# Seven block products in place of eight for one quad of k-tiles in layer A's input projection

## The chip, the cores and the metric

The kernel runs on one core of a Trainium2 chip. Its time is device microseconds for one execution; three runs of the kernel before gave 1843.43 to 1845.11 us, median 1844.06.

## The reference, cut to what matters

A trunk of two layers on 256 rows of 2048 numbers, all in float32. The change lies in the first part of layer A:

```python
h = rms_norm(x, a_norm[layer])                     # (1, 256, 2048)
q, k, v, g = jnp.split(h @ a_w_in[layer], 4, axis=-1)   # a_w_in: (2048, 16384)
o = chunked_relbias_attention(split_heads(q), split_heads(k), split_heads(v), rel_bias)
x = x + (o * jax.nn.silu(g)) @ a_w_out[layer]      # 32 heads of 128
```

Layer B follows with two more projections of 2048 to 8192, its own attention and a projection back.

## The kernel before, in words

**Products in three parts.** A float32 product is made of three matmuls on fp32r operands. Both factors are split into a high part (the value rounded to fp32r) and a low part (the rest): h·hi, h·lo and l·hi are summed in PSUM (`mm3`, line 160). The stationary operand is a 128x128 block of the transposed activations (`xTh`, `xTl`), the moving one a 128x512 block of weights.

**Units and pairs.** The projection's columns are cut into units of 512, and the 256 rows into NT = 2 tiles, so a unit has two accumulators of one PSUM bank each. Layer A has 16 pairs of units, one for two heads each: `aqk` (q and k of the two heads) and `avg` (v and gate). A unit runs over 16 k-tiles of 128, two to a step (KB = 2): 8 steps of 12 matmuls.

**The feed.** `Feed` (line 171) brings weights to TensorE. SP loads a step's weights (128 x 2 x 512, 512 KB) into one of three `raw` buffers; ScalarE copies it to `hi` (line 216), VectorE subtracts to get `lo` (line 217). `hi` and `lo` have four buffers each, and `get` prepares three steps ahead: the `hi` of a step can be written when TensorE is done with the step four before it.

**Attention beside the products.** While one pair is multiplied, the attention of the pair before it advances in pieces between the steps (`drive`, line 519, with QK_STEPS and PV_STEPS: at which step how many pieces). Its pieces in order: the evacuation of `aqk` to `qk`; a transpose by 32x32 blocks on VectorE into `qkY` and 16 DMAs from there to `qkZ`, issued by GpSimd (`turn`, line 321); the splits `wideh`/`widel` and `q1h`/`q1l` (lines 344, 345); the scores `s1p` and `s0p` on TensorE, at the end of the `avg` unit; softmax (lines 378 to 388); the scaled gate and a second `turn` (`sgY`, `sgZ`); the split of the probabilities, again `wideh`/`widel`; the products `op` (lines 349 to 351 and 405); `oT`, and its split into `oAh` and `oAl`, the stationary operand of the output projection.

Before, the second split comes with the last step of the next pair's `aqk` unit, and `op` after the first step of that pair's `avg` unit. `qkZ` and `sgZ` share one buffer, `qkY` and `sgY` another.

**What sets the order.** The code says what depends on what; a scheduler then orders each engine's instructions by its own estimate of times, so that instructions can stand far from where the code has them. On the chip ScalarE, VectorE, SP and GpSimd each take theirs in that order; one that waits holds up all behind it.

## Time and profile before

| | |
|---|---|
| median of 3 runs | 1844.06 us |
| the profiled execution's own time | 1843.38 us |
| its span, first to last instruction | 1841.7 us |
| TensorE, matmuls | 8387, busy 1830.1 us |
| VectorE | busy 1121.7 us |
| ScalarE | busy 1005.6 us |
| GpSimd | busy 543.5 us, nearly all in issuing DMAs |
| DMA | 396.31 MB, mean 215 GB/s |

A row of a timeline has start and length in us, engine, line, instruction, out<-in, shape, how often, and in brackets the idle time of the engine before it with what ended it. Matmuls overlap each other, so the length of one is not what it costs; for that a stretch of many is divided by their number. Names lose the number of the pair: `aqk_lo` is the low part of any step of any `aqk` unit.

### The profile page before, as it was taken

What the parts mean: (1) busy time and instruction counts of PE and PEld (TensorE: products, weight loads), DVE (VectorE), ACT (ScalarE), POOL (GpSimd) and SP (SyncE); (2) the same over time, 40 slices, a digit from 0 to 9 for tenths busy, and PEclk for the clock granted to TensorE, in tenths of its full rate; (3) what the DMA queues carried; (4) which work ended last, traced back from release to release, by engine and by line L of the source; (5) the groups of instructions that cost most, each with busy time, mean ns of one, the idle gap of its engine ahead of it and who ended that gap; (6) DMA issues with size and microseconds to landing.
All of it is one profiled execution on the core that took longest, in us unless ns stands there. A gap on an engine that the chain in (4) does not pass through costs nothing.

```text
span 1841.7 us, 25094 instructions
## 1 busy us (share of the span) xinstructions
PE 1830.1 (99%) x8387; PEld 1523.0 (83%) x8387; DVE 1121.7 (61%) x1433; ACT 1005.6 (55%) x1695; POOL 543.5 (30%) x1127
## 2 busy tenths in 40 slices
PE   9999999999999999999999999999999999999998
PEld 7888888888888888888888888888888888888886
DVE  6666666666666666556655566666665666665654
ACT  6555555555555555454546565555555655554443
POOL 1333333333333333111103333333333333333000
PEclk9999999999999999999999999999999999999999
DMA  7766666666767666677756666666766766677664
GB/s 255 235 217 214 212 214 215 214 213 212 216 214 214 215 214 214 209 226 227 230 190 220 214 216 213 214 214 215 217 212 213 220 213 210 215 237 220 206 205 161
DMA packets 142241, 396.31 MB, mean 215 GB/s; under 512 B 31104, under 2 KB 35744, under 8 KB 141984
## 3 DMA queue, kind: packets, MB, share of 16 engines
q1 hardware_dynamic: 106960, 354.25, 61.6%
q0 software_dynamic: 34048, 39.13, 6.5%
q8 instruction: 66, 1.08, 0.3%
q10 hardware_dynamic: 1104, 1.34, 0.2%
q14 instruction: 63, 0.52, 0.1%
HBM read 351.05 MB, written 4.23 MB: 193 GB/s over the span
## 4 chain that ended last, share of the span: by engine, by line
PE 97%; DVE 1%; DMA 1%; ACT 0%; issue 0%; ACTq 0%; SPq 0%; DVEq 0%
PE bkv_acc L168 19%; PE bqg_acc L168 19%; PE avg_acc L168 18%; PE aqk_acc L168 18%; PE bo_acc L168 9%; PE ao_acc L168 9%; PE op L405 1%; PE s0p L371 1%; PE op L351 0%; PE s1p L351 0%; PE s1p L350 0%; PE op L350 0%; PE op L349 0%; PE s1p L349 0%; DMA avg_raw<-in_a_w_in 0%; DMA xr<-in_x_t 0%
## 5 line engine op out<-in xcount | busy, mean ns | idle before, releaser
L330 POOL DMA_DIRECT2D sgZ<-sgY x512 | 251.5, 498 | 435.2 <-DVE sgY L326 364.1
L330 POOL DMA_DIRECT2D qkZ<-qkY x504 | 247.9, 499 | 399.1 <-DVE vl L424 147.2
L217 DVE TENSOR_TENSOR bqg_lo<-bqg_raw,bqg_hi 128x1024 fp32r<-128x1024 f32 x128 | 156.0, 1222 | 121.3 <-ACT bqg_hi L216 121.3
L217 DVE TENSOR_TENSOR avg_lo<-avg_raw,avg_hi 128x1024 fp32r<-128x1024 f32 x127 | 154.0, 1219 | 110.8 <-ACT avg_hi L216 105.4
L217 DVE TENSOR_TENSOR bkv_lo<-bkv_raw,bkv_hi 128x1024 fp32r<-128x1024 f32 x128 | 155.6, 1219 | 87.6 <-ACT bkv_hi L216 87.6
L216 ACT ACTIVATE bqg_hi<-bqg_raw 128x1024 fp32r<-128x1024 f32 x128 | 135.3, 1058 | 128.3 <-PE bqg_acc L168 67.8
L217 DVE TENSOR_TENSOR aqk_lo<-aqk_raw,aqk_hi 128x1024 fp32r<-128x1024 f32 x125 | 151.5, 1219 | 84.6 <-ACT aqk_hi L216 84.5
L168 PE MATMUL aqk_acc<-aqk_hi,xTh 128*128 128x512 f32 x512 | 195.8, 392 | 0.5 <-ACT aqk_hi L216 0.5
L168 PE MATMUL bkv_acc<-bkv_hi,xkvh 128*128 128x512 f32 x512 | 195.7, 392 | 0.0
L168 PE MATMUL avg_acc<-avg_hi,xTh 128*128 128x512 f32 x512 | 195.7, 392 | 0.0
L168 PE MATMUL bqg_acc<-bqg_hi,xbh 128*128 128x512 f32 x512 | 195.5, 392 | 0.0
L216 ACT ACTIVATE avg_hi<-avg_raw 128x1024 fp32r<-128x1024 f32 x127 | 133.1, 1057 | 113.3 <-PE avg_acc L168 54.2
L168 PE MATMUL aqk_acc<-aqk_lo,xTh 128*128 128x512 f32 x512 | 194.1, 389 | 0.5 <-DVE aqk_lo L217 0.5
L168 PE MATMUL avg_acc<-avg_lo,xTh 128*128 128x512 f32 x512 | 194.1, 389 | 0.4 <-DVE avg_lo L217 0.4
L168 PE MATMUL bkv_acc<-bkv_hi,xkvl 128*128 128x512 f32 x512 | 194.4, 390 | 0.0
L168 PE MATMUL aqk_acc<-aqk_hi,xTl 128*128 128x512 f32 x512 | 194.4, 390 | 0.0
L168 PE MATMUL bqg_acc<-bqg_hi,xbl 128*128 128x512 f32 x512 | 194.3, 390 | 0.0
L168 PE MATMUL avg_acc<-avg_hi,xTl 128*128 128x512 f32 x512 | 194.3, 390 | 0.0
L168 PE MATMUL bkv_acc<-bkv_lo,xkvh 128*128 128x512 f32 x512 | 194.1, 389 | 0.0
L168 PE MATMUL bqg_acc<-bqg_lo,xbh 128*128 128x512 f32 x512 | 194.1, 389 | 0.0
L216 ACT ACTIVATE bkv_hi<-bkv_raw 128x1024 fp32r<-128x1024 f32 x128 | 134.8, 1057 | 76.2 <-PE bqg_acc L168 61.3
L216 ACT ACTIVATE aqk_hi<-aqk_raw 128x1024 fp32r<-128x1024 f32 x125 | 131.0, 1056 | 81.4 <-PE aqk_acc L168 40.1
(188 smaller groups left out, 3430.3 us busy)
## 6 DMA issues: line engine op xcount, KB each, us to landing
bqg_raw<-in_b_w_in SPq DMA_DIRECT2D x128, 512.0 KB, 4.2
bkv_raw<-in_kv_w SPq DMA_DIRECT2D x128, 512.0 KB, 3.5
avg_raw<-in_a_w_in SPq DMA_DIRECT2D x127, 512.0 KB, 4.3
aqk_raw<-in_a_w_in SPq DMA_DIRECT2D x125, 512.0 KB, 3.8
ao_raw<-in_a_w_out SPq DMA_DIRECT2D x64, 512.0 KB, 4.4
bo_raw<-in_b_w_out SPq DMA_DIRECT2D x64, 512.0 KB, 4.2
sgZ<-sgY POOLq DMA_DIRECT2D x512, 40.0 KB, 4.0
qkZ<-qkY POOLq DMA_DIRECT2D x504, 32.0 KB, 3.3
```

Source lines behind the costliest of these rows:

```text
L168: pe.matmul(acc[t], x[:, t * P:(t + 1) * P], w, start=k == 0 and i == 0, stop=k == nk - 1 and i == 2)
L216: act.activation(hi[:, j], raw[:, j], AF.Copy)
L217: self.splits.append(dve.tensor_sub(lo[:, j], raw[:, j], r32(hi[:, j])))
L330: queues[j % 2].dma_start(out=z[j * SQ:(j + 1) * SQ, i], in_=y[i * SQ:(i + 1) * SQ, j])
L371: pe.matmul(s0p[:, i], q0[:, i], qkT[:, HG + i, 0], start=True, stop=True)
L405: pe.matmul(op[:, i, P:], v1[:, i * DH:(i + 1) * DH], pT[:, i, NT], start=False, stop=i == HG - 1)
```

## The change

From the second pair on, the last step's two k-tiles are taken out of both units of a pair, which run over 7 steps each. The 2x2 blocks left over (2 row tiles by 2 k-tiles, times 2 k-tiles by 2 units) are multiplied by Strassen's scheme in Winograd's form: 7 block products, 21 matmuls, where 8 products took 24.

- `sums_of_x` (once, after the first pair) makes four sums and differences of the activations' blocks and splits them (`sums`).
- `Feed` gets an item `quad` between the third and fourth step of `aqk`: two DMAs bring the two units' weights into `quad_raw` (one buffer), three subtractions on VectorE make `quad_t`, and four splits follow, of 1024, 1024, 512 and 1024 columns, into the same `hi` and `lo` buffers. `quad_raw` and `quad_t` are named `quad_101` and `quad_102` in the order.
- `quad` issues the products: two go straight into the `aqk` accumulators, one into the first `avg` accumulator, four into banks `p1`, `p5`, `p7`, `p6`. ScalarE and VectorE combine those into `comb`, and ScalarE scales two rows of it.
- The evacuation of `aqk` adds `comb` and moves from ScalarE to VectorE. `close_vg` adds the other two rows of `comb` to the `avg` accumulators on VectorE; v and gate are then read from `comb`.
- The attention's pieces move: the split of the probabilities to the sixth step, `op` and `oT` to the end of the `aqk` unit. In the first `turn` of every pair but the first ScalarE issues 4 of the 16 DMAs.
- `comb`, `sums`, `quad_raw` and `quad_t` take the buffers of the early loads and of the squares.

```diff
+QK7_STEPS = {0: 1, 5: 1, 6: 2}
+PV7_STEPS = {0: 1, 5: 1, 6: 2}
...
+            if spec == "quad":
+                for r in range(2):
+                    sp.dma_start(out=quad_raw[:, r], in_=a_w_in[2 * b + r][QUAD])
+                self.loaded += [(spec, i, None, (None, None)) for i in range(4)]
...
+        def quad(self, i):
+
+            raw, t = quad_raw, quad_t
+            if not i:
+                dve.tensor_sub(t[:, 0], raw[:, 1], raw[:, :, 0])
+                dve.tensor_sub(t[:, 1, 0], raw[:, 1, 1], t[:, 0, 0])
+                dve.tensor_sub(t[:, 1, 1], raw[:, 0, 1], t[:, 1, 0])
+            src = [raw[:, 0], t[:, 0], raw[:, 1, 1:], t[:, 1]][i]
...
+            act.activation(hi[:, :n], src, AF.Copy)
+            dve.tensor_sub(lo[:, :n], src, r32(hi[:, :n]))
...
-                queues[j % 2].dma_start(out=z[j * SQ:(j + 1) * SQ, i], in_=y[i * SQ:(i + 1) * SQ, j])
+                queues[j].dma_start(out=z[j * SQ:(j + 1) * SQ, i], in_=y[i * SQ:(i + 1) * SQ, j])
...
+    def quad(qk, vg):
...
+        p1, p5, p7, p6 = (bank(n) for n in ("p1", "p5", "p7", "p6"))
+        w = feed.get()
+        prod(p1, x(0, 0), w, 0, True)
+        prod(qk.acc[0], x(1, 0), w, 1, False)
+        w = feed.get()
+        prod(p5, sx(0), w, 0, True)
+        prod(p7, sx(2), w, 1, True)
+        w = feed.get()
+        dot3(vg.acc[0], sx(3), [v[:, 0] for v in w], True, False)
+        vg.begun.add(0)
+        w = feed.get()
+        prod(p6, sx(1), w, 0, True)
+        prod(qk.acc[1], x(1, 1), w, 1, False)
+        act.activation(comb[:, 0], p1, AF.Copy)
+        dve.tensor_add(comb[:, 3], comb[:, 0], p6)
+        dve.tensor_add(comb[:, 2], comb[:, 3], p5)
+        dve.tensor_add(comb[:, 1], comb[:, 3], p7)
+        dve.tensor_add(comb[:, 3], comb[:, 1], p5)
+        for t in range(NT):
+            act.activation(comb[:, t], comb[:, t], AF.Copy, scale=rsA[:, t:t + 1])
...
+                dve.scalar_tensor_tensor(qk[:, t], accs["qk"][t], rsA[:, t:t + 1], comb[:, t],
+                                         op0=OP.mult, op1=OP.add)
...
+                dve.tensor_add(comb[:, NT + t], accs["vg"][t], comb[:, NT + t])
...
-            accs["qk"], vg = drive(unit(xT), prev, PV_STEPS), unit(xT)
+            accs["quad"] = True
+            first, second = (Unit(xT, next(order)) for _ in range(2))
+            accs["qk"] = drive(rest(first), prev, PV7_STEPS, (QUAD_STEP - 1, lambda: quad(first, second)))
+            vg = rest(second)
...
-        old, prev = prev, side_a(g, accs)
+        finish(prev)
+        prev = side_a(g, accs)
         advance(prev)
-        accs["vg"] = drive(vg, prev, QK_STEPS if g else {0: 1, 5: 1, 6: 2}, old=old)
+        accs["vg"] = drive(vg, prev, QK7_STEPS)
```

The first place is VectorE where the `aqk` unit of the seventh pair ends and its `avg` unit begins. `widel<-sgZ` is the low part of the sixth pair's probabilities, `avg_lo` are the first steps of the `avg` unit, L250 is the last of the three subtractions for the eighth pair's quad, L597 the new evacuation. Before:

```order
L217 TENSOR_TENSOR aqk_lo_2740<-aqk_raw_2689,aqk_hi_2739 128x1024
L217 TENSOR_TENSOR avg_lo_2758<-avg_raw_2707,avg_hi_2757 128x1024
L217 TENSOR_TENSOR avg_lo_2776<-avg_raw_2725,avg_hi_2775 128x1024
L345 TENSOR_TENSOR widel<-sgZ,wideh 128x256 x2
L217 TENSOR_TENSOR avg_lo_2794<-avg_raw_2743,avg_hi_2793 128x1024
L326 STREAM_TRANSPOSE qkY<-qk 128x1024
L217 TENSOR_TENSOR avg_lo_2826<-avg_raw_2761,avg_hi_2825 128x1024
L217 TENSOR_TENSOR avg_lo_2878<-avg_raw_2779,avg_hi_2877 128x1024
L409 TENSOR_TENSOR oT<-op,sgZ 128x256 x2
```

And VectorE at the same place in the changed kernel:

```order
L579 TENSOR_TENSOR comb<-comb,p_2825 128x512
L230 TENSOR_TENSOR avg_lo_2897<-avg_raw_2854,avg_hi_2896 128x1024
L230 TENSOR_TENSOR avg_lo_2915<-avg_raw_2863,avg_hi_2914 128x1024
L382 TENSOR_TENSOR widel<-sgZ,wideh 128x256 x2
L250 TENSOR_TENSOR quad_102<-quad_101,quad_102 128x512
L597 SCALAR_TENSOR_TENSOR qk<-aqk_acc_2743,rstd_a,comb 128x512
L230 TENSOR_TENSOR avg_lo_2939<-avg_raw_2882,avg_hi_2938 128x1024
L446 TENSOR_TENSOR oT<-op,sgZ 128x256 x2
L597 SCALAR_TENSOR_TENSOR qk<-aqk_acc_2744,rstd_a,comb 128x512
L230 TENSOR_TENSOR avg_lo_2977<-avg_raw_2900,avg_hi_2976 128x1024
L451 TENSOR_TENSOR oAl_180<-oT,oAh_176 128x512
L363 STREAM_TRANSPOSE qkY<-qk 128x1024
```

Two `avg_lo` stand ahead of `widel` in both; `oT` now precedes `qkY`, and five other rows lie between `widel` and `qkY` beside it.

The second place is ScalarE at the same point of the program, where `wideh<-sgZ` is the high part of the same probabilities and needs the DMAs into `sgZ`. Before:

```order
L216 ACTIVATE aqk_hi_2739<-aqk_raw_2689 128x1024
L216 ACTIVATE avg_hi_2757<-avg_raw_2707 128x1024
L216 ACTIVATE avg_hi_2775<-avg_raw_2725 128x1024
L344 ACTIVATE wideh<-sgZ 128x256 x2
L216 ACTIVATE avg_hi_2793<-avg_raw_2743 128x1024
```

And ScalarE at that place in the changed kernel:

```order
L229 ACTIVATE aqk_hi_2878<-aqk_raw_2842 128x1024
L581 ACTIVATE comb<-comb,rstd_a 128x512
L381 ACTIVATE wideh<-sgZ 128x256 x2
L229 ACTIVATE avg_hi_2896<-avg_raw_2854 128x1024
L229 ACTIVATE avg_hi_2914<-avg_raw_2863 128x1024
L581 ACTIVATE comb<-comb,rstd_a 128x512
L229 ACTIVATE avg_hi_2938<-avg_raw_2882 128x1024
```

`wideh` has moved from behind the first two `avg_hi` to ahead of them, while on VectorE `widel` is still behind the two `avg_lo` that are made from them. The rows are alike in 13 of the 15 pairs.

The third place is VectorE around the quad of the seventh pair in the changed kernel; `quad_lo` are its splits, and L248 and L249 make `quad_102` for the quad of the eighth pair:

```order
L256 TENSOR_TENSOR quad_lo_2793<-quad_102,quad_hi_2792 128x1024
L363 STREAM_TRANSPOSE sgY<-sg 128x1280
L256 TENSOR_TENSOR quad_lo_2809<-quad_101,quad_hi_2808 128x512
L256 TENSOR_TENSOR quad_lo_2829<-quad_102,quad_hi_2828 128x1024
L230 TENSOR_TENSOR aqk_lo_2839<-aqk_raw_2645,aqk_hi_2838 128x1024
L248 TENSOR_TENSOR quad_102<-quad_101 128x1024
L230 TENSOR_TENSOR aqk_lo_2851<-aqk_raw_2663,aqk_hi_2850 128x1024
L230 TENSOR_TENSOR aqk_lo_2860<-aqk_raw_2695,aqk_hi_2859 128x1024
L576 TENSOR_TENSOR comb<-comb,p_2827 128x512
L249 TENSOR_TENSOR quad_102<-quad_101,quad_102 128x512
```

The subtractions, which the code has just ahead of the first split of their own quad, have moved nearly a whole pair ahead, into the quad before.

More of the change, by code (lines that the diff above doesn't have):

```diff
@@ L168, in mm3 @@
             pe.matmul(acc[t], x[:, t * P:(t + 1) * P], w,
-                      start=k == 0 and i == 0, stop=k == nk - 1 and i == 2)
+                      start=t not in begun, stop=k == nk - 1 and i == 2)
+            begun.add(t)
     class Feed:
@@ L205, in prepare @@
             spec, b, raw, (before, behind) = self.loaded.pop(0)
+            if spec == "quad":
+                self.quad(b)
+                self.refill()
+                return
             if before:
@@ L220, in prepare, with refill @@
             self.ready.append((hi, lo))
-            while ahead and len(self.loaded) < RAW:
+            if ahead:
+                self.refill()
+        def refill(self):
+            while sum(raw is not None for _, _, raw, _ in self.loaded) < RAW:
                 n = len(self.loaded)
@@ L511, in vg @@
             return accs["v"], accs["g"]
-        yield from attention(g, biases, qk, vg, halfA, oA, (pool, pool) if g else (pool, act))
+        yield from attention(g, biases, qk, vg, halfA, oA, (pool, pool, pool, act) if g else (pool, act, pool, act))
     def close_vg(accs):
+        if "quad" in accs:
+            for t in range(NT):
+                dve.tensor_add(comb[:, NT + t], accs["vg"][t], comb[:, NT + t])
+            accs["vg"] = [comb[:, NT + t] for t in range(NT)]
         accs["v"] = v_split(accs["vg"], 0, rsA)
```

67 lines of the change are left out of this document (53 added, 14 removed).

## The prediction

> **What bounds the kernel now.** I read the page first, then the clock by core, the waits of TensorE, the chain in order of time, and last the timelines of the engines around one pair of layer A.
>
> ```profile
> PE 1830.1 (99%) x8387; PEld 1523.0 (83%) x8387; DVE 1121.7 (61%) x1433; ACT 1005.6 (55%) x1695; POOL 543.5 (30%) x1127
> core 0: 1841.7 us, clock 0.999
> PE heat L98 <- DVE zeros L95: 1.3, 1, 1.3
> PE aqk_acc L168 <- ACT aqk_hi L216: 0.5, 1, 0.5
> PE aqk_acc L168 <- DVE aqk_lo L217: 0.5, 1, 0.5
> PE avg_acc L168 <- DVE avg_lo L217: 0.4, 1, 0.4
> ```
>
> TensorE is busy all the time at full clock, and the four waits listed add up to 2.7 us. So it is the bound: a matmul less is worth its time, and every wait that the change brings to TensorE is paid in full. The price of one matmul is not its duration. The first row below is the page's group (mean 392 ns), the others are pieces of the chain, each with its start and its length.
>
> ```profile
> L168 PE MATMUL aqk_acc<-aqk_hi,xTh 128*128 128x512 f32 x512 | 195.8, 392 | 0.5 <-ACT aqk_hi L216 0.5
> 282.32 0.45 PE s0p L371 x4
> 282.77 21.81 PE aqk_acc L168 x96
> 308.01 0.45 PE op L405 x4
> 308.46 19.09 PE avg_acc L168 x84
> 328.26 0.45 PE s0p L371 x4
> 374.19 0.45 PE s0p L371 x4
> ```
>
> 96 matmuls take 21.81 us, so one is worth 0.2272 us; the 392 ns overlap each other. A pair of units takes 45.93 us (328.26 to 374.19, from one s0p piece to the next).
>
> **What is removed.** Each of the 15 pairs from the second on makes 7 products of three matmuls in place of 8: 3 fewer a pair, 45 in all, and 45 x 0.2272 = 10.2 us. Nothing lies beside them, so all of it comes off the end if nobody waits. [...]
>
> **What is added, and where it lies.** On VectorE, per pair: three subtractions (L248 to L250), 1.5 more splits of 1024 columns, four additions into comb, two in close_vg, and the two evacuations that ScalarE did. By the 1.16 us of half a row x2 and the 0.68 and 0.69 us of the 512-column rows below, that is 1.16 + 2 x 0.69 + 1.5 x 1.16 + 8 x 0.68 = 9.7 us in a pair of 45.2. VectorE is 61% busy, some 28 us a pair, so it fits on average: 38 of 45. ScalarE gains about as much as it loses. Averages therefore allow the 10.2 us; the order decides. The rows are of one pair, VectorE first, then ScalarE, then TensorE and GpSimd.
>
> ```profile
> 283.36 0.68 DVE L378 SCALAR_TENSOR_TENSOR sg<-s1p,tb 128x512 f32<-128x512 f32 x1
> 289.17 1.51 DVE L326 STREAM_TRANSPOSE sgY<-sg 128x1280 f32<-128x1280 f32 x1
> 304.59 0.76 DVE L345 TENSOR_TENSOR widel<-sgZ,wideh 128x256 fp32r<-128x256 f32 x2 [3.09 <-ACT wideh L344]
> 307.00 1.25 DVE L326 STREAM_TRANSPOSE qkY<-qk 128x1024 f32<-128x1024 f32 x1
> 308.17 2.32 DVE L217 TENSOR_TENSOR avg_lo<-avg_raw,avg_hi 128x1024 fp32r<-128x1024 f32 x2
> 310.40 0.75 DVE L409 TENSOR_TENSOR oT<-op,sgZ 128x256 f32<-128x256 f32 x2
> 311.85 0.69 DVE L414 TENSOR_TENSOR oAl<-oT,oAh 128x512 fp32r<-128x512 f32 x1 [0.70 <-ACT oAh L413]
> ...
> 278.28 0.72 ACT L344 ACTIVATE wideh<-qkZ 128x256 fp32r<-128x256 f32 x2 [3.68 <-DMA qkZ<-qkY]
> 304.14 0.72 ACT L344 ACTIVATE wideh<-sgZ 128x256 fp32r<-128x256 f32 x2 [3.90 <-DMA sgZ<-sgY]
> 304.77 1.04 ACT L216 ACTIVATE avg_hi<-avg_raw 128x1024 fp32r<-128x1024 f32 x1
> 306.86 2.00 ACT L216 ACTIVATE avg_hi<-avg_raw 128x1024 fp32r<-128x1024 f32 x2
> 323.19 0.72 ACT L344 ACTIVATE wideh<-qkZ 128x256 fp32r<-128x256 f32 x2 [2.65 <-DMA qkZ<-qkY]
> ...
> 281.45 0.28 PE L349 MATMUL s1p<-wideh,q1h 128*128 128x256 f32 x1
> 307.13 0.28 PE L349 MATMUL op<-wideh,vh 128*128 128x256 f32 x1
> 307.25 0.28 PE L350 MATMUL op<-widel,vh 128*128 128x256 f32 x1
> ...
> 291.23 4.41 POOL L330 DMA_DIRECT2D sgZ<-sgY  x9 [6.55 <-PE aqk_acc L168]
> 299.29 1.48 POOL L330 DMA_DIRECT2D sgZ<-sgY  x3 [0.58 <-DMA sgZ<-sgY]
> 311.77 7.93 POOL L330 DMA_DIRECT2D qkZ<-qkY  x16 [11.00 <-PE avg_acc L168]
> ```
>
> Call E the start of the first s1p matmul (281.45). Before, the op products come at E+25.7. Their chain starts with the transpose sgY (E+7.7), whose sixteen DMAs GpSimd issues until 300.77; ScalarE waits 3.90 us for sgZ and splits it at W = E+22.7 (wideh), VectorE follows within 0.45 us (widel, done at 305.35). That is 1.8 us before op: hidden, but closely.
>
> **The edit that costs.** In the changed order wideh stands ahead of the two avg_hi splits on ScalarE, and on VectorE widel stands behind both avg_lo. Both engines run in order, so avg_hi and avg_lo, which were done before sgZ came, now wait for sgZ, and widel waits for them. From W: the first avg_hi starts at W+0.63 (304.77 less 304.14), ends at W+1.67, the second at about W+2.63; two avg_lo take 2.32 from W+1.70, so widel starts at W+4.02, and its first half, which the second op matmul reads, ends at W+4.4. Before it was W+0.8. And op comes sooner: it stands directly behind the aqk unit, and three matmuls are gone, so it is due at E+25.7 - 0.7 = E+25.0, its second matmul at E+25.1. TensorE waits there for (W-E) + 4.4 - 25.1 = (W-E) - 20.7, and everything behind op on TensorE waits too.
>
> With this pair's W that is 2.0 us. Here s1p starts 0.87 us ahead of the s0p piece (281.45, 282.32); so the next two E are 327.39 and 373.32. At the second of them sgZ is early:
>
> ```profile
> 366.60 0.73 ACT L344 ACTIVATE wideh<-qkZ 128x256 fp32r<-128x256 f32 x2
> 379.97 1.51 DVE L326 STREAM_TRANSPOSE sgY<-sg 128x1280 f32<-128x1280 f32 x1
> 393.88 0.73 ACT L344 ACTIVATE wideh<-sgZ 128x256 fp32r<-128x256 f32 x2 [1.78 <-DMA sgZ<-sgY]
> ```
>
> There qkZ was split at E-6.7 without a wait, sgY came at E+6.7 and W at E+20.6: no wait at op. So from sgY to W it takes 13.9 to 15.0 us, and sgY is late where qkZ is late. What will qkZ be in the changed kernel? From widel's end (W+4.8) VectorE has L250, the first evacuation, an avg_lo, oT, the second evacuation, an avg_lo, oAl and qkY: 0.69 + 0.68 + 1.16 + 0.75 + 0.68 + 1.16 + 0.69 + 1.25 = 7.1, so W+11.9. GpSimd starts 0.55 later (290.68 to 291.23) and issues 12 DMAs, not 16, at 7.93 / 16 = 0.496: W+18.4; ScalarE got qkZ 3.5 after the last issue (319.70 to 323.19): W+21.9. The next E lies 20.14 behind the second op matmul (327.39 less 307.25; 84 matmuls then as now), at W+24.5. So qkZ comes at E-2.6, late as in the first pair (E-3.2), in every pair: the delay feeds itself. sgY then stands at the first pair's E+7.7, plus 0.6 for qkZ, plus two close_vg additions ahead of it on VectorE (1.36), less about 0.65, because the first quad's ScalarE split runs ahead of the tanh and not between: E+9.0. W = E+9.0+14.45 = E+23.45, and op waits 2.75 us.
>
> The sum: 14 pairs by 2.75 are 38.5 us (the last pair of layer A has its wideh and widel rows mixed in between, and no next quad; I count none for it), less 10.2: +28.3 on the profiled execution's 1843.38, which is 0.7 under the median of the runs: 1872. Bounds: sgY at E+8.1 (the early pair's 6.7 and the additions) and 13.9 give 1.3 a pair in 14 pairs, +8; sgY at E+9.5 and 15.0 give 3.8 in 15 pairs, +47.
>
> **The other edits.** L248 of the next pair stands between this pair's quad and the next aqk_lo, and waits for the second half of the next quad's weights. That load can go out only when the quad's third split is done:
>
> ```profile
> aqk_raw<-in_a_w_in SPq DMA_DIRECT2D x125, 512.0 KB, 3.8
> DMA to landing us min/median/max: 3.1/3.8/8.2
> 35.91 0.60 ACTq L330
> ```
>
> sgY E+9.0 to 10.5, the split of 512 columns to 11.2, load landed at 15.1, L248 to 16.3, aqk_lo to 17.5; TensorE wants it 69 matmuls (three steps, the quad, one step) and the first of the next behind s1p and s0p, which take 1.14 (25.68 to op less 108 x 0.2272): at E+17.05. So about 0.45 us late, but op's wait behind it shrinks by the same, since W doesn't move: it costs nothing of its own up to a landing of 6.1 us. Held behind L248 are the aqk_lo of the next steps and the comb additions, which nobody on TensorE awaits so soon; held behind the load on SP is aqk raw6, for a product two steps (5.5 us) further on. The four qk DMAs on ScalarE cost 4 x 0.60 = 2.4 us in a place where it is three steps (8.2 us) ahead. The quad's own splits are ready 0.5 to 1.5 us ahead of their products by the same walk. sums_of_x (once, at most six 512-column rows, 6 x 0.69 = 4.1 us of VectorE) hides behind the first three steps of pair two, or lengthens one op wait by 4.1; I take 0, nearest to the cover of 8.2.
>
> **Rivals.** That the matmuls don't go is none: the order has 45 rows fewer. One, sgZ comes in time: W at or below E+20.7 in every pair, and the 10.2 us are had whole: 1833. For it: the pair at 393.88 and averages that fit. Against it: W+21.9 above, by which qkZ is late even when only W is late, and the two additions. Two, half of that: the wait is 0.7 us a pair and eats the saving, 1843. Three, the weights of the next quad land late: at the maximum of 8.2 us aqk_lo is 4.8 late, 2.1 more than op's wait, in 14 pairs +29 on top: 1901; it decides from 6.1 us on, and the median speaks against it. Four, TensorE comes out of each wait at a lower clock: if the step of twelve behind it went at half speed, that is 2.7 a pair, 14 x 2.7 = 38, 1910. No run here shows it: no listed wait of TensorE is over 1.3 us, and the clock is 0.999. [...]
>
> **How the numbers follow.** My forecast, op waiting 1.4 to 3.8 us a pair: 0.70. Rival one 0.13, two 0.06, three 0.06, four 0.05. A measurement of this kernel tells about 0.2% from no change. Faster by more: 0.13 plus the lower edge of rival two, 0.14; within: 0.05; slower: 0.81. The range 1848 to 1892 holds my case nearly whole, leaves out rival one, most of two and three.
>
> **What would show it.** Right: TensorE waits on widel (L387) at about 2.75 us in each pair, wideh(sgZ) near E+23.5, a pair of 48 us, 8342 matmuls at 0.227. Wrong: no such wait and a pair of 45.2 us (rival one); waits on aqk_lo behind L248 that are longer than on widel (three); a granted clock under 0.99 in layer A (four). If sgY stands at E+7 the loop through qkZ was mis-drawn.

## The result, and the profile after

The changed kernel takes 1899.76 us (median of 5 runs, 1896.00 to 1901.01), the kernel before 1845.04 beside it: a ratio of 1.0289, 95% interval 1.0270 to 1.0309. The forecast was 1872, with a range up to 1892. So the direction was right and the size was not: 55 us slower, where 28 were forecast.

From the page of the changed kernel, the busy times and the chain that ended last, by engine:

```profile
PE 1845.6 (97%) x8342; PEld 1527.0 (81%) x8342; DVE 1249.9 (66%) x1634; ACT 1036.0 (55%) x1741; POOL 513.9 (27%) x1067
...
PE 62%; DMA 4%; POOL 2%; issue 2%; ACT 1%; DVE 1%; ACTq 0%; DVEq 0%; POOLq 0%
```

Its clock:

```profile
core 0: 1894.3 us, clock 0.990
```

Its waits of TensorE (what waited, for what: us in total, times, longest):

```profile
PE op L387 <- DVE widel L382: 31.4, 14, 3.6
PE aqk_acc L172 <- DVE aqk_lo L230: 3.3, 6, 0.7
PE avg_acc L172 <- ACT avg_hi L229: 1.8, 1, 1.8
```

The 45 matmuls are gone. In their place TensorE waits at `op`, 14 times, for `widel`, and VectorE is busy 128 us more than before. Lines moved by the change: 217 is now 230, 326 is 363, 330 is 367, 344/345 are 381/382, 349 is 386.

The timelines of one pair, VectorE, ScalarE, TensorE, GpSimd:

```profile
602.91 1.51 DVE L363 STREAM_TRANSPOSE sgY<-sg 128x1280 f32<-128x1280 f32 x1
608.87 1.23 DVE L248 TENSOR_TENSOR quad<-quad 128x1024 f32<-128x1024 f32 x1 [1.60 <-DMA quad<-in_a_w_in]
619.82 2.36 DVE L230 TENSOR_TENSOR avg_lo<-avg_raw,avg_hi 128x1024 fp32r<-128x1024 f32 x2 [3.32 <-ACT avg_hi L229]
622.09 0.75 DVE L382 TENSOR_TENSOR widel<-sgZ,wideh 128x256 fp32r<-128x256 f32 x2
628.22 1.24 DVE L363 STREAM_TRANSPOSE qkY<-qk 128x1024 f32<-128x1024 f32 x1
652.91 1.51 DVE L363 STREAM_TRANSPOSE sgY<-sg 128x1280 f32<-128x1280 f32 x1
...
618.11 0.72 ACT L381 ACTIVATE wideh<-sgZ 128x256 fp32r<-128x256 f32 x2 [2.96 <-DMA sgZ<-sgY]
618.74 1.99 ACT L229 ACTIVATE avg_hi<-avg_raw 128x1024 fp32r<-128x1024 f32 x2
641.25 0.73 ACT L381 ACTIVATE wideh<-qkZ 128x256 fp32r<-128x256 f32 x2 [3.59 <-DMA qkZ<-qkY]
...
593.71 0.28 PE L386 MATMUL s1p<-wideh,q1h 128*128 128x256 f32 x1
622.57 0.39 PE L387 MATMUL op<-widel,vh 128*128 128x256 f32 x1 [2.93 <-DVE widel L382]
644.51 0.28 PE L386 MATMUL s1p<-wideh,q1h 128*128 128x256 f32 x1
...
630.08 4.40 POOL L367 DMA_DIRECT2D qkZ<-qkY  x9 [15.24 <-DVE qkY L363]
635.44 0.51 POOL L367 DMA_DIRECT2D qkZ<-qkY  x1 [0.97 <-DMA qkZ<-qkY]
636.54 0.98 POOL L367 DMA_DIRECT2D qkZ<-qkY  x2 [0.60 <-DMA qkZ<-qkY]
```

This is the queue that the prediction described: `wideh` waits 2.96 us for `sgZ`, both `avg_hi` come behind it, both `avg_lo` behind those, `widel` last, and `op` behind `widel`. W, the start of `wideh` of sgZ, is E+24.4 here (618.11 less 593.71) and E+23.6 in the mean of the pairs, where E+23.45 was forecast.

**Four links.** Read the same rows as a ring: from `sgY` (602.91) to W (618.11), from W to `qkY` (628.22), from `qkY` to the split of qkZ (641.25), from there to the next `sgY` (652.91). Four such links fill a period by definition, so their sum proves nothing. What tells is which of them is rigid. In the changed kernel the last link is 11.65 or 11.66 us in all 15 pairs, and the second 10.10 or 10.11 in the first 14, while the time from TensorE's `s1p` to `sgY` wanders from 6.6 to 9.9. So `sgY` follows the ring and not TensorE. Between `widel` and `qkY`, in the second link, stand six rows of VectorE beside `oT`, not five as said with the order above. In the other two links the splits wait for the DMAs: `wideh` has a wait ahead of it in all 15 pairs, at both splits. Before, the last link was 10.9 us in nine of the 15 pairs and longer in the other six, up to 13.4, where `sgY` came 6.65 or 6.66 us behind `s1p`: whichever was later, and neither held TensorE up, for the period is 45.93 us in every pair.

Means in us, from the starts of these rows, over 14 pairs from the second `s1p` on; the last column is the range of the fourth link over all 15:

| kernel | time | pair | sgY to W | W to qkY | qkY to split of qkZ | split of qkZ to sgY |
|---|---|---|---|---|---|---|
| before | 1844 to 1845 | 45.93 | 14.57 | 3.13 | 16.51 | 10.89 to 13.44 |
| changed | 1899.8 | 49.22 | 14.82 | 9.94 | 12.76 | 11.65 to 11.66 |
| move_alone | 1847.3 | 46.11 | 14.46 | 3.10 | 14.56 | 12.66 to 15.65 |
| hi_first | 1863.1 | 47.23 | 15.98 | 6.82 | 12.80 | 11.64 to 11.66 |
| fill_wait | 1910.8 | 49.87 | 15.08 | 10.75 | 12.43 | 11.65 to 11.66 |
| op_late | 1889.6 | 48.94 | 14.93 | 8.71 | 13.69 | 11.64 to 11.66 |
| sg_on_act | 1879.9 | 48.40 | 16.42 | 8.08 | 12.42 | 11.46 to 11.65 |
| subs_early | 1890.3 | 49.03 | 15.34 | 5.98 | 12.67 | 11.65 to 15.45 |
| qk_on_pool | 1877.2 | 48.10 | 16.17 | 6.79 | 14.56 | 10.51 to 10.59 |
| loop_cut | 1881.4 | 48.39 | 18.88 | 4.51 | 13.30 | 11.64 to 11.66 |
| subs_gap | 1850.3 | 45.91 | 15.20 | 6.70 | 12.56 | 11.64 to 11.66 |
| op_late_held | 1860.5 | 46.85 | 16.02 | 5.60 | 13.53 | 11.65 to 11.66 |
| all_in | 1853.2 | 46.44 | 15.02 | 5.47 | 14.34 | 11.64 to 11.66 |
| z_freed | 1853.1 | 46.13 | 15.12 | 5.32 | 12.06 | 13.72 to 14.03 |
| subs_gap_z | 1864.5 | 47.06 | 15.16 | 6.56 | 12.46 | 12.78 to 13.15 |
| changed_z | 1894.4 | 48.84 | 14.83 | 8.85 | 12.35 | 12.78 to 12.92 |
| start_held | 1850.4 | 46.26 | 15.18 | 6.64 | 12.81 | 11.65 to 11.66 |
| qk_early | 1838.2 | 45.39 | 16.08 | 5.08 | 12.33 | 11.65 to 12.57 |

TensorE's own work for a pair of the changed kernel is 45.25 us (45.93 less three times 0.2272).

**Where the 52.6 us of the spans went** (1894.3 less 1841.7): the first `s1p` starts at 56.18 and not 51.78, 4.4 us; the 15 periods from there to the last `s1p` add up to 734.35 us and not 689.0, 45.3 more; what follows is 2.8 longer. Forecast for the 15 periods was +28.3.

### The profile page after: what moved, and what is told of

Same layout as the page of the kernel before. It is cut to its first block, busy times and chain, and to the rows that moved or that the text cites. A ratio compares the mean times of both kernels' runs of the same rounds, so it can differ in the third digit from the quotient of the medians.

```text
span 1894.3 us, 25382 instructions
## 1 busy us (share of the span) xinstructions
PE 1845.6 (97%) x8342; PEld 1527.0 (81%) x8342; DVE 1249.9 (66%) x1634; ACT 1036.0 (55%) x1741; POOL 513.9 (27%) x1067
## 4 chain that ended last, share of the span: by engine, by line
PE 62%; DMA 4%; POOL 2%; issue 2%; ACT 1%; DVE 1%; ACTq 0%; DVEq 0%; POOLq 0%
PE bkv_acc L172 17%; PE bqg_acc L172 17%; PE ao_acc L172 9%; PE bo_acc L172 9%; PE avg_acc L172 4%; DMA sgZ<-sgY 2%; PE aqk_acc L172 1%; POOL sgZ L367 1%; DMA qkZ<-qkY 1%; PE op L442 1%; PE s0p L408 0%; POOL qkZ L367 0%; DMA quad<-in_a_w_in 0%; DMA avg_raw<-in_a_w_in 0%; ACT avg_hi L229 0%
## 5 line engine op out<-in xcount | busy, mean ns | idle before, releaser
L367 POOL DMA_DIRECT2D qkZ<-qkY x444 | 217.8, 498 | 480.7 <-DVE vl L461 151.0
L230 DVE TENSOR_TENSOR avg_lo<-avg_raw,avg_hi 128x1024 fp32r<-128x1024 f32 x112 | 134.2, 1216 | 90.3 <-ACT avg_hi L229 90.3
L172 PE MATMUL avg_acc<-avg_hi,xTh 128*128 128x512 f32 x452 | 178.0, 406 | 1.8 <-ACT avg_hi L229 1.8
L172 PE MATMUL avg_acc<-avg_hi,xTl 128*128 128x512 f32 x452 | 174.9, 399 | 0.0
L172 PE MATMUL aqk_acc<-aqk_lo,xTh 128*128 128x512 f32 x452 | 171.6, 391 | 3.3 <-DVE aqk_lo L230 3.3
L172 PE MATMUL avg_acc<-avg_lo,xTh 128*128 128x512 f32 x452 | 173.9, 397 | 0.8 <-DVE avg_lo L230 0.8
L172 PE MATMUL aqk_acc<-aqk_hi,xTh 128*128 128x512 f32 x452 | 173.1, 394 | 0.3 <-ACT aqk_hi L229 0.3
L172 PE MATMUL aqk_acc<-aqk_hi,xTl 128*128 128x512 f32 x452 | 171.2, 390 | 0.0
L229 ACT ACTIVATE aqk_hi<-aqk_raw 128x1024 fp32r<-128x1024 f32 x110 | 112.8, 1052 | 81.1 <-DMA aqk_raw<-in_a_w_in 52.2
L230 DVE TENSOR_TENSOR aqk_lo<-aqk_raw,aqk_hi 128x1024 fp32r<-128x1024 f32 x110 | 131.9, 1221 | 33.7 <-ACT aqk_hi L229 33.5
```

The source lines that it names most:

```text
L172: pe.matmul(acc[t], x[:, t * P:(t + 1) * P], w, start=t not in begun, stop=k == nk - 1 and i == 2)
L229: act.activation(hi[:, j], raw[:, j], AF.Copy)
L230: self.splits.append(dve.tensor_sub(lo[:, j], raw[:, j], r32(hi[:, j])))
L367: queues[j].dma_start(out=z[j * SQ:(j + 1) * SQ, i], in_=y[i * SQ:(i + 1) * SQ, j])
```

## The experiments

The theory that the first four runs were made to test was the prediction's own: the pair is as long as TensorE's work and its waits. Its rivals were the clock behind each wait, and `op`'s new place alone. Where a number below is called the ring's, it is read from the table.

**move_alone**: `op`'s new place, in the kernel before, without the seven products.

```diff
-PV_STEPS = {0: 1, 7: 1}
+PV_STEPS = {0: 1, 6: 1, 7: 2}
...
-        old, prev = prev, side_a(g, accs)
+        finish(prev)
+        prev = side_a(g, accs)
```

> The kernel before, with nothing but op and oT moved to the end of the aqk unit (eight steps and eight products as before); on ScalarE wideh stays behind the first two avg_hi. Theory (the place of wideh costs, the move alone doesn't): op due at E+22.9 us, sgZ split at E+21 us, no wait over 0.3 us in most pairs, time within 0.5% of the kernel before, 1840 to 1853. Rival (moving op up costs by itself): waits of 1 to 2 us a pair, 1860 to 1880.

Measured 1847.29 us, ratio 1.0015 (1.0006 to 1.0025). One pair of 48.35 us, the others 45.9 to 46.0. The new place alone costs nearly nothing.

**hi_first**: in the changed kernel, sgZ's split is held behind the newest `avg_hi` on ScalarE, in layer A; nothing else is touched.

```diff
-        ph, pl = split([pT[:, i, :NT] for i in range(HG)], "wide")
+        with tc.issue_after(feed.newest.ins) if len(queues) > 3 and queues[3] is act else nullcontext():
+            ph, pl = split([pT[:, i, :NT] for i in range(HG)], "wide")
```

> The changed kernel with one order edge: on ScalarE the split wideh of sgZ may not stand ahead of the newest weight split, so in every pair it comes behind the two avg_hi instead of ahead of them; on VectorE nothing moves. Theory (the two avg_hi and avg_lo that were put behind sgZ make widel late, the waits at op let the clock drop): widel ends about 0.9 us after sgZ lands instead of 4.4, op's second product waits under 0.5 us a pair instead of 2.24, the clock in layer A goes back to 1.00, and the time falls by the 31 us of waits and some 14 us of slow matmuls to 1850 (1845 to 1860). Rival A (sgZ itself comes too late for an op that was moved up): waits of 1 us or more a pair stay, time above 1870. Rival B (the slow matmuls have another cause than the waits): waits gone, avg_acc means still 397 to 406 ns, time about 1865.

Measured 1863.1 us, ratio 1.0101 (1.0086 to 1.0116): this one edge in ScalarE's order gave back 37 of the 55 us. In the two traces, 34 us apart, 28 are in the 15 periods; 4.1 are a start that came sooner though the edge does not touch it (below). The time is above the 1845 to 1860 that were expected; near rival B's 1865, but its sign is missing, for the `avg` matmuls are back at 392 ns. The wait at `op` nearly went (first its row among the waits, then three rows of the timeline), and yet 18 us stayed:

```profile
PE op L387 <- DVE widel L382: 3.9, 12, 0.7
```

```profile
593.81 1.06 ACT L229 ACTIVATE avg_hi<-avg_raw 128x1024 fp32r<-128x1024 f32 x1 [0.52 <-DMA avg_raw<-in_a_w_in]
595.39 0.71 ACT L381 ACTIVATE wideh<-sgZ 128x256 fp32r<-128x256 f32 x2
602.17 1.24 DVE L363 STREAM_TRANSPOSE qkY<-qk 128x1024 f32<-128x1024 f32 x1
```

The listed waits of TensorE in this kernel add up to 14 us over the whole span, and a pair is 2 us over 45.25. The rest fits the ring: from W to `qkY` it is 6.8 us, 3.7 more than before. The hold has a price of its own, too. In none of the 15 pairs does `wideh` wait for sgZ; it stands behind the second `avg_hi`, which waits for its weights (rows above), and by the landing times in the trace sgZ was complete 1.1 to 2.0 us before W in 13 of the 15. That is the 1.2 us by which the first link is longer than in the changed kernel.

**fill_wait**: ten bf16 matmuls on a tile of zeros ahead of `op` in 15 pairs (they feed nothing), to keep TensorE busy where it waits; `qkY` held behind `oAl`, and `oT` two rows later.

```diff
+        if fill:
+            warm = bank("warm")
+            for i in range(FILL):
+                pe.matmul(warm, zeros[0][:, :P], zeros[0][:, P:], start=i == 0, stop=i == FILL - 1)
...
+        with tc.issue_after(behind[0].ins) if behind and name == "qk" else nullcontext():
+            dve.transpose(y, src.rearrange("p n (j u) -> p j n u", u=SQ))
```

> The changed kernel with ten dummy bf16 matmuls of 512 columns on zeros ahead of op in each of the 15 pairs, 2.2 us of TensorE work about as long as its mean wait there; on VectorE oT moves two rows back. Theory (TensorE's idleness ahead of op lets the clock drop): op comes no sooner, waits on widel shrink to under 1 us because the dummies fill them, the granted clock of layer A's pairs is 0.99 to 1.00, avg_acc means go back to 390 to 393 ns, and though 34 us of dummy work are added the time falls by 8 to 16 us to 1880 to 1890. Rival (the matmuls behind op are slow because of contention with VectorE and ScalarE catching up, or the drop is not tied to idling): the means stay at 397 or above and the time is 1896 or more.

Measured 1910.8 us, ratio 1.0359 (1.0341 to 1.0377): the expectation failed (and its rival had the means of the matmuls wrong). The clock did come back, from 0.990 to 0.997, and the `avg` matmuls fell from 406 to 394 ns, but the pair became 0.65 us longer. The first row is of the changed kernel, the other two of fill_wait.

```profile
L172 PE MATMUL avg_acc<-avg_hi,xTh 128*128 128x512 f32 x452 | 178.0, 406 | 1.8 <-ACT avg_hi L229 1.8
```

```profile
L176 PE MATMUL avg_acc<-avg_hi,xTh 128*128 128x512 f32 x452 | 172.9, 394 | 1.4 <-ACT avg_hi L233 1.4
L445 PE MATMUL warm<-zeros 128*128 128x512 bf16 x150 | 35.0, 380 | 0.0
```

The link from W to `qkY` grew by 0.81 us, with `oT` later and `qkY` behind `oAl`, and the pair nearly as much. `op` still waits for `widel` there (9.1 us in 11 pairs), so the added matmuls did not hold it up. So the low clock is real, and nothing here shows it setting the end: TensorE loses that time beside a ring that is longer anyway. This run made the ring the theory.

**op_late**: in the changed kernel, `op` back behind the first `avg` step, where it was before.

```diff
-PV7_STEPS = {0: 1, 5: 1, 6: 2}
+PV7_STEPS = {0: 1, 6: 1}
...
-        finish(prev)
-        prev = side_a(g, accs)
+        old, prev = prev, side_a(g, accs)
```

> The changed kernel with op back at its old place, behind the first avg step (PV steps 0 and 6, the rest in the next unit); the rows of wideh ahead of avg_hi stay. Theory (the place of wideh on ScalarE is what costs, not op's place): TensorE now waits at the first avg step, for avg_hi by 0.5 to 1.5 us and then for avg_lo, 1 to 2.5 us a pair together, and less or not at all at op; time 1870 to 1900. Rival (op was moved up too far and that alone costs): no waits over 0.3 us a pair and 1845 to 1855.

Measured 1889.6 us, ratio 1.0246 (1.0230 to 1.0261). `op` nearly waits no more (0.5 us), and TensorE waits 12.3 us at `s1p` for qkZ's split and 7.8 for `aqk_lo` in place of it, not at the first `avg` step as expected: the time is within its range, the wait moved to another point of the same ring.

**sg_on_act**, **subs_early**, **qk_on_pool** and **loop_cut** each change one link of hi_first, the ring's theory against the sum of listed waits.

Of sg_on_act:

```diff
-        z = turn(sg, HG * NB + NT * HG, "sg")
+        z = turn(sg, HG * NB + NT * HG, "sg", (pool, pool, pool, queues[3]))
```

Of subs_early, around L248 to L250:

```diff
+            with nullcontext() if i else tc.issue_after(self.splits[-1].ins):
```

Of qk_on_pool:

```diff
-..., (pool, pool, pool, act) if g else (pool, act, pool, act))
+..., (pool, pool, pool, pool) if g else (pool, act, pool, act), True)
```

loop_cut is sg_on_act with the edit of op_late.

> The kernel of hi_first, and four of the sixteen DMAs of sgZ issued by ScalarE in place of GpSimd in layer A. Theory (each pair lasts as long as the longer of TensorE's own work, 45.25 us, and the closed way of the attention from one sgY over sgZ's split, qkY, qkZ's split and the softmax to the next sgY, 47.2 us in hi_first): sgY to wideh(sgZ) falls from 16.0 to about 13.4, the way to 44.6, the pair to 45.3, the time from 1863 to about 1836 (1830 to 1846). Rival (the time is the sum of the waits that TensorE's rows show, 12.6 us in hi_first): only the op waits of 5.2 us go, so about 1858. If the four DMAs hold up ScalarE's splits, TensorE waits for quad_lo or aqk_lo 1 to 2 us a pair, and the time stays at 1855 to 1870.

> The kernel of hi_first, and the three subtractions L248 to L250 held behind the last aqk_lo ahead of the quad, where the code makes them; in the order they then stand ahead of sgY and no longer between the aqk_lo behind it. Theory (the pair is as long as the attention's closed way): they and one or two quad_lo lengthen qkZ's split to sgY from 11.65 to about 15 us, less 0.7 between sgZ's split and qkY; the pair goes from 47.2 to about 50, the time from 1863 to about 1900 (1885 to 1915), though no instruction is added. Rival (the sum of TensorE's waits): the waits on aqk_lo (4.8 us) go with the wait of L248 for its weights, so about 1858.

> The kernel of hi_first, and all sixteen DMAs of qkZ issued by GpSimd from the second pair on, as before the change. Theory (closed way): qkY to wideh(qkZ) grows from 12.8 by four issues, 2 us, the pair to 49.2, the time from 1863 to about 1891 (1880 to 1900). Rival (qkZ was split 2.1 us ahead of s1p in hi_first, so 2 us are hidden): 1863 to 1868.

> The kernel of sg_on_act, and op moved behind the first avg step, so that qkY stands three VectorE rows behind sgZ's split and not eight. Theory (closed way): 13.4 + 3 + 12.8 + 11.65 = 41 us, well under TensorE's 45.25, so TensorE is the bound again: pairs of 45.25 to 45.5, time 1828 to 1842, faster than the kernel before by up to 0.8%, with what is lost at the start (about 4 us) left. Rival (the sum of waits): the waits of op_late move to s1p and aqk_lo as there, 10 to 20 us, time 1845 to 1860.

Measured: 1879.9 (ratio 1.0198, 1.0180 to 1.0215), 1890.3 (1.0250, 1.0235 to 1.0266), 1877.2 (1.0177, 1.0160 to 1.0194) and 1881.4 (1.0203, 1.0188 to 1.0219). The sum of listed waits failed in subs_early and qk_on_pool: 1858 and at most 1868 by that theory. The ring's direction held in both (subs_early lies in its range, qk_on_pool 3 us under it). In subs_early, where the three subtractions stand ahead of `sgY`, the fourth link went to 14.98 us in most pairs, as worked out. In qk_on_pool the third link grew by the 1.8 us, but the scheduler also put an `aqk_lo` ahead of qkZ's split, so that the fourth became 1.1 shorter: 14 us were paid and not 28.

The ring failed as a forecast in sg_on_act and loop_cut (1836 and 1828 to 1842), and so did the sum of waits (1858 and 1845 to 1860). I had drawn the ring with one way into W. These are ScalarE's timeline and a wait of TensorE in sg_on_act:

```profile
643.65 2.45 ACTq L367 DMA_DIRECT2D sgZ<-sgY  x4
655.45 1.06 ACT L229 ACTIVATE avg_hi<-avg_raw 128x1024 fp32r<-128x1024 f32 x1 [1.25 <-DMA avg_raw<-in_a_w_in]
658.10 0.71 ACT L381 ACTIVATE wideh<-sgZ 128x256 fp32r<-128x256 f32 x2
```

```profile
PE p L387 <- DVE quad_lo L256: 10.6, 14, 0.8
```

`wideh` does not wait for sgZ there (no bracket), as it did not in hi_first; it stands behind two `avg_hi`, and the first of those waits for its weights. The four DMAs did what they were meant to: by the landing times sgZ was complete 11.0 to 11.7 us behind `sgY` in 11 of 15 pairs, where hi_first took 13.7 to 15.6. W did not follow. The four DMAs, 2.45 us on ScalarE, also held up its `quad_hi`, and TensorE waits at the quad's products (10.6 us). In loop_cut, with `op` later in the code, the newest `avg_hi` was the third, and sgY to W became 18.9 us. A hold is a link of its own.

**subs_gap**, **op_late_held**, **all_in**: the three subtractions put where VectorE idles, behind `qkY` (held behind the sixth-newest weight split); in op_late_held, op_late with the hold at the second `avg_hi` and the first quad's load held back; all_in is both.

subs_gap, on hi_first, around L248 to L250:

```diff
+            with nullcontext() if i else tc.issue_after(self.splits[-6].ins):
```

op_late_held, on op_late:

```diff
+        with tc.issue_after(feed.his[-2].ins) if len(queues) > 3 and queues[3] is act else nullcontext():
+            ph, pl = split([pT[:, i, :NT] for i in range(HG)], "wide")
...
+                with tc.issue_after(self.last.ins) if b == 1 else nullcontext():
                     for r in range(2):
                         sp.dma_start(out=quad_raw[:, r], in_=a_w_in[2 * b + r][QUAD])
```

> The kernel of hi_first, and the three subtractions L248 to L250 held behind an avg_lo, so that they stand between qkY and the split of qkZ, where VectorE idled 3 to 6 us in the runs before; nothing else moved. Theory (a pair lasts as long as the closed way over VectorE's and ScalarE's orders and the weights' loads, TensorE's 45.25 us being shorter): the way loses L250 (0.7 us) between sgZ's split and qkY and the wait of L248 among the aqk_lo (1.3 us), so pairs of 45.5 to 46.3 and 1838 to 1850. Rival (only the listed waits count): the waits on aqk_lo, 4.8 us, go: 1858.

> The changed kernel, op moved behind the first avg step, sgZ's split on ScalarE held behind the second avg_hi (not the third, as loop_cut had it), all sixteen DMAs of sgZ on GpSimd, and the first quad's load held back behind the three aqk loads ahead of it. Theory: sgY to wideh(sgZ) back at 15 to 16 us (in loop_cut 18.9, by the third avg_hi), from there to qkY 5 to 6, so the way is 45 to 46 us: pairs of 45.3 to 46, 3 to 4 us less at the start: 1836 to 1846. Rival (loop_cut's 48.4 came from op's place and not from the hold): 1870 to 1880.

> The kernel of op_late_held, and the three subtractions held between oT and the split of qkZ as in subs_gap. Theory: from wideh(sgZ) to qkY 4 to 4.5 us, the way 43 to 44.5, under TensorE's 45.25; so TensorE is the bound again, its waits under 0.3 us a pair: 1830 to 1838, the 10.2 us less than before that 45 matmuls are worth, less 0 to 4 at the start. Rival (the way through the weights' loads holds pairs at 46 and above whatever stands in VectorE's order): 1845 to 1855.

Measured: 1850.3 (1.0028, 1.0017 to 1.0040), 1860.5 (1.0092, 1.0077 to 1.0107), 1853.2 (1.0048, 1.0031 to 1.0064). subs_gap came out at the edge of what was expected: moving three small rows out of the way took 13 us off hi_first, though TensorE's listed waits on what stood behind them were 4.8. (In the two traces the 15 periods are 18.5 us shorter and the start is 5.8 later.) op_late_held missed both its ranges. all_in missed too, and lies in its rival's (1845 to 1855, pairs of 46 and above). One thing that was missing is in all_in's timelines of VectorE and GpSimd:

```profile
593.86 1.24 DVE L364 STREAM_TRANSPOSE qkY<-qk 128x1024 f32<-128x1024 f32 x1
596.40 0.75 DVE L448 TENSOR_TENSOR oT<-op,sgZ 128x256 f32<-128x256 f32 x2
597.77 5.38 POOL L368 DMA_DIRECT2D qkZ<-qkY  x11 [12.17 <-DVE oT L448]
```

`qkY` is done at 595.10, but GpSimd starts only when `oT` has read sgZ: qkZ and sgZ are one buffer. So the ring also runs from W over `op` and `oT` to the DMAs of qkZ, and `op` later on TensorE makes it longer.

**z_freed**, **subs_gap_z**, **changed_z**: in layer A qkZ takes the buffer of `qk` instead; in all_in, in subs_gap (with the first quad's load held back), and in the changed kernel.

```diff
-    z = turn(qk.rearrange("p t (c d) -> p (t c) d", d=DH), NT * 2 * HG, "qk", queues)
+    z = turn(..., "qk", queues, "R" if queues[3] is act else "Z")
```

> The kernel of all_in, and qkZ in layer A put into the buffer of qk (dead once qkY is made, and next needed by sg) in place of sgZ's. In all_in the DMAs of qkZ wait for oT, the last reader of sgZ, and so for op: qkY to wideh(qkZ) was 14.3 us against 12.5. Theory (the closed way runs over that shared buffer): qkY to wideh(qkZ) falls to 12 to 12.7, the way to 44 to 44.7, under TensorE's 45.25: pairs of 45.3 to 45.6, time 1830 to 1840, faster than the kernel before. Rival (14.3 is GpSimd's own issue and landing): still 46.4 a pair, 1850 to 1855.

> The kernel of subs_gap (op not moved), with qkZ in the buffer of qk and the first quad's load held back behind the three aqk loads ahead of it. Theory: here oT stands ahead of qkY on VectorE, so the buffer frees nothing: the way stays 45.5 to 45.9 as in subs_gap, and only the start's 3 to 4 us come off: 1843 to 1848. Rival (the shared buffer costs in this order too): pairs of 45.3, 1835 to 1841.

> The changed kernel with only qkZ put into the buffer of qk; the order that follows has one avg_hi and not two behind sgZ's split, both avg_lo still ahead of widel. Theory: sgY to wideh(sgZ) 14.8, from there to qkY 8 to 9 (three rows fewer), 12.4, 11.65: pairs of 47 to 48, 1862 to 1880. Rival (the buffer itself was the cost of the change): pairs under 46, under 1850.

Measured: 1853.1 (1.0049, 1.0034 to 1.0064), 1864.5 (1.0114, 1.0098 to 1.0130), 1894.4 (1.0285, 1.0264 to 1.0305). All three missed; z_freed's time lies in its rival's range. The third link fell to 12.06 in z_freed as worked out, so its 14.3 was the buffer; but the fourth grew from 11.65 to 13.7 at once (12.8 in the other two). VectorE's order shows how: in all three a `quad_lo` has moved ahead of `sg`, whose rows come 1.13 us later for it, and in z_freed an `aqk_lo` also stands between the two rows of `widel` (0.95 us). No row waits ahead of `sg`. Why the scheduler moved them with the buffer, these runs do not show. The buffer moved the cost around the ring.

**qk_early** and **start_held**, both on subs_gap: the first takes rows out of the second link without a new sharing, the second changes only the first quad's load.

```diff
-QK7_STEPS = {0: 1, 5: 1, 6: 2}
+QK7_STEPS = {5: 1, 6: 2}
...
+                with tc.issue_after(self.turned.ins) if self.turned and nm[:3] == 'avg' else nullcontext():
                     self.splits.append(dve.tensor_sub(lo[:, j], raw[:, j], r32(hi[:, j])))
...
+        feed.tail = 1
         finish(prev)
         prev = side_a(g, accs)
-        advance(prev)
+        advance(prev, 2)
+        if callable(feed.tail):
+            feed.tail()
```

(`turned` is the newest transpose; `tail` makes `oAh` and `oAl`. qkZ's split is held behind the second-newest weight split in the same way, and the first quad's load as in op_late_held.)

> The kernel of subs_gap (buffers as in the changed kernel), and: the turn of qk made ahead of the next avg step and those avg_lo behind it held behind qkY, oAh and oAl made behind qkY, sgZ's and qkZ's splits held behind the weights' splits that stood ahead of them, the first quad's load held behind the three aqk loads ahead of it. VectorE's rows between sgZ's split and qkY are then widel, one avg_lo, two evacuations and oT: 4.2 us and not 6.7. Theory (the closed way): 15.2 + 4.2 + 12.3 + 11.65 = 43.4 us, under TensorE's 45.25, so TensorE is the bound in every pair: pairs of 45.3 to 45.5, time 1830 to 1838, faster than the kernel before. Rival (each row that is taken out of the way lengthens another part of it, as in z_freed): pairs of 45.9 to 46.4, 1846 to 1853.

> The kernel of subs_gap, and the first quad's load held behind the three aqk loads ahead of it; nothing else. In subs_gap the first s1p matmul came 6.1 us later than before the change, with a wait of 2.7 us for avg_hi. Theory (the first quad's two loads of 512 KB stand among those of the first avg unit): the first s1p matmul back at 52 us, the second pair up to 2 us longer because L248 then waits, pairs of 45.9 else: 1843 to 1847. Rival (the start is late for another reason): 1848 to 1852.

qk_early measured 1838.2 us, ratio 0.9967 (0.9954 to 0.9980): the seven products do pay, 0.33% under the kernel before and at the upper edge of what was expected. Its page (busy times, chain by engine):

```profile
PE 1823.4 (99%) x8342; PEld 1515.1 (83%) x8342; DVE 1257.1 (68%) x1634; ACT 1040.5 (57%) x1741; POOL 512.7 (28%) x1067
...
PE 95%; DMA 2%; ACT 1%; DVE 1%; issue 0%; POOL 0%; SPq 0%; DVEq 0%; ACTq 0%; POOLq 0%
```

Its longest waits in layer A:

```profile
PE p L389 <- DVE quad_lo L258: 1.1, 1, 1.1
PE op L388 <- ACT wideh L383: 0.6, 1, 0.6
```

Two pieces of its chain in order of time, a pair apart:

```profile
599.50 0.45 PE s0p L411 x4
644.76 0.45 PE s0p L411 x4
```

And the links of that pair in the timeline:

```profile
605.40 1.51 DVE L365 STREAM_TRANSPOSE sgY<-sg 128x1280 f32<-128x1280 f32 x1
621.41 0.71 ACT L383 ACTIVATE wideh<-sgZ 128x256 fp32r<-128x256 f32 x2
626.47 1.23 DVE L365 STREAM_TRANSPOSE qkY<-qk 128x1024 f32<-128x1024 f32 x1
640.64 0.72 ACT L383 ACTIVATE wideh<-qkZ 128x256 fp32r<-128x256 f32 x2 [3.61 <-DMA qkZ<-qkY]
```

VectorE does the work of the changed kernel (7 us more of it, in a span 58 us shorter), the waits are nearly gone, and TensorE is 95% of the chain, where it was 62%. The pair shown is 45.26 us from one s0p to the next, and ten of the 15 periods are 45.25 or 45.26. `sgY` is 6.77 us behind `s1p` in ten of 15 pairs, and the fourth link wanders again: TensorE sets the pace. Of the 10.2 us, 5.2 arrived in the span: the second period is 47.98 (2.7 lost at the first quad), the others lose 2.0 together.

start_held measured 1850.35 us, ratio 1.0033 (1.0022 to 1.0045), no faster than subs_gap and in its rival's range, though not for the rival's reason. The first `s1p` came back from 57.87 to 51.49 us as expected, but the next period became 48.07 for 45.25, and the mean of the rest 0.35 longer. So in these two traces the sooner start was given back. They are one execution each of kernels whose ten runs lie 11 and 12 us apart, so that the 0.35 may be chance.

## Why the prediction was wrong in size

- **What is removed**: right. 8342 matmuls, and in qk_early, with the waits nearly gone, ten of the 15 periods are 0.68 us shorter than before, which is three matmuls of 0.2272. All 15 together are 5.5 us shorter, not 10.2.
- **"The edit that costs"**: right, and shown by hi_first, where undoing it alone took the wait away. The order of `wideh`, `avg_hi`, `avg_lo`, `widel` and the wait at `op` came as told; W to the second `op` matmul is 4.46 us, forecast 4.4.
- **The step that failed** is the loop through qkZ: "GpSimd starts 0.55 later ... and issues 12 DMAs, not 16, at 7.93 / 16 = 0.496: W+18.4; ScalarE got qkZ 3.5 after the last issue". From `qkY`'s end to the split I had 10.0 us; the mean is 11.5 (12.76 less 1.24). The quoted GpSimd rows show why: nine DMAs go out without a gap, then GpSimd waits 0.97 and 0.60 us for earlier DMAs of the same turn, so issuing takes 7.44 us (630.08 to 637.52) and not 5.95, and the split comes 3.7 behind it. Over the 15 pairs issuing takes 6.5 to 8.8 us, mean 7.4. The 7.93 that the price came from is one pair's, and near the lowest of the kernel before (7.84 to 11.24, mean 8.6). The prediction's own row of sgZ has such a wait: 16 DMAs from 291.23 to 300.77, by which 12 would take 7.2. Of the other links W to `qkY` was 0.7 shorter than forecast and sgY to W 0.4 longer. Together 1.2 us more in the ring, and a ring pays in every pair: 14 x 1.2 = 17 us, the 45.3 in place of 28.3.
- **The price was put in the wrong place.** I reckoned TensorE's time as work plus the wait at `op`. The listed wait is 2.24 us a pair (31.4 / 14), less than the 2.75 forecast, and still the pair was 3.97 over 45.25: of the other 24 us in 14 pairs some 15 are the half clock behind the waits (30.7 us of it, last section), some 3 the listed waits for `aqk_lo`, and what is left was not listed. My own ring gave the pair (48.0); its wait was only one of the places where TensorE's loss shows.
- **"The other edits" cost nothing of their own**: wrong. L248 to L250 cost 13 us beside hi_first's order. How they reach the ring (late `aqk_lo`, so late free buffers, so late weights ahead of W) fits the rows but was only argued. The start was not in the sum at all, and 4.4 us go there: TensorE waits for an `avg_hi` that stands on ScalarE behind eight DMAs of the first `turn`, and these took 7.58 us to issue, where before they took 5.33. The first quad's two loads, which stand among those of the first `avg` unit, are a candidate: in the six kernels where they are held back the first `s1p` comes at 51.3 to 52.6 us. But in the others it comes anywhere from 52.1 to 57.9, and in hi_first, with the same order of loads, at 52.05 with the eight DMAs issued in 5.35. So the loads alone do not make it. Of the 2.8 us behind the last `s1p` 1.7 lie in two periods of layer B, 47.03 and 46.53 us for 45.93, which most other runs lack; why stays open.

```profile
30.39 0.42 SPq L201 DMA_DIRECT2D quad<-in_a_w_in  x1
34.76 0.43 SPq L201 DMA_DIRECT2D quad<-in_a_w_in  x1
36.41 7.58 ACTq L367 DMA_DIRECT2D qkZ<-qkY  x8
44.11 2.96 ACT L229 ACTIVATE avg_hi<-avg_raw 128x1024 fp32r<-128x1024 f32 x3 [8.06 <-DMA avg_raw<-in_a_w_in]
45.22 0.50 PE L172 MATMUL avg_acc<-avg_hi,xTh 128*128 128x512 f32 x1 [1.75 <-ACT avg_hi L229]
56.18 0.28 PE L386 MATMUL s1p<-wideh,q1h 128*128 128x256 f32 x1
```

- **Rival one** (1833) is what the products are worth: qk_early gets half-way there, in another order. **Rival three**, late weights: no, `aqk_lo` waits 3.3 us in all. **Rival four**, the lower clock: it is there (0.990 over the span, 0.999 before), as the last section shows, and in fill_wait (0.997) the end did not come sooner with most of it gone.

## What to carry to other kernels

Where side work goes through engines that take their instructions in order (in the changed kernel both `avg_hi` stood behind a `wideh` that waited 2.96 us) and comes back to itself (here: transpose, DMA, split, transpose, DMA, split), draw it as a ring and price each link, over all rounds and not from one; in these runs the period followed the ring where the ring was longer than TensorE's work (49.22 us in the changed kernel for 45.25), and TensorE's work else (45.25 or 45.26 in ten periods of qk_early), and an error in a link was paid in every round (1.2 us, 14 times). To tell which of the two rules, look for the interval that is the same to 0.01 us in every round (11.65 or 11.66 in the changed kernel's fourth link). Waits of the busiest engine only said where it stood when the ring was late, and removing one moved it (in op_late to 0.5 us at `op` and 12.3 at `s1p`); take rows out of the ring instead, and check that a hold, a shared buffer or a load does not close it another way.

## What the hardware showed that I had not expected

In the trace of the changed kernel the granted clock halved beside each of the seven waits at `op` of 2.30 us and more. Stretches around the `op` wait quoted above (start:end, length, then busy time and count of PE, PEld, DVE, ACT and POOL, granted clock, DMA share, GB/s):

```profile
619.00:622.00 3.00, 0.64 (x4) 0.29 (x2) 2.19 (x2) 3.00 (x4) 0.00 (x0) 1.00 0.00 0
622.00:625.00 3.00, 2.43 (x13) 2.08 (x14) 3.00 (x6) 0.77 (x2) 0.00 (x0) 0.84 0.87 249
625.00:628.00 3.00, 3.00 (x10) 2.37 (x9) 3.00 (x6) 1.23 (x3) 0.00 (x0) 0.59 0.73 253
628.00:631.00 3.00, 3.00 (x15) 2.49 (x14) 2.56 (x3) 1.04 (x1) 0.92 (x2) 1.00 0.58 203
```

Here the clock is full during the wait, which ends at 622.57. The trace has full and half speed (1.0 and 0.5) as the only two values, so 0.84 of one stretch and 0.59 of the next put the slow time at about 624.0 to 627.5: it begins 1.4 us behind the wait and lasts 3.4. The clock fell so at eight of the 13 waits at `op` from 129 to 723 us: at all seven of 2.30 us and more, at one of 1.99, and not at those of 2.14, 2.01 and less. At the other seven it began from 0.8 us before the end of the wait to 1.5 behind it, and once it lasted 6.8. The slow times began at 129.09, 180.29, 279.28, 378.26, 473.84, 624.02, 671.81 and 723.01. Why the wait of 1.99 us had one beside it and that of 2.14 none, no run shows.

Not all that TensorE loses is listed as a wait. From 110 to 750 us the starts of all_in's matmuls, less 0.2272 us for one of 512 columns and 0.1136 for the others (0.45 for four), show 17 us lost, where the listed waits come to 4.5 (before: 0.6 and none). A row of a matmul of 512 columns is 0.39 us long and the next starts 0.23 behind it; by that, an estimate, up to 0.16 us of a late start leaves no idle time to list. A stretch is checked by the starts, not by the waits alone.
